# All chunks of an mLSTM moved from among the linear-attention tiles to among the later projection pairs, with six more SBUF units for temporaries

## The chip, the cores and the metric

The kernel runs on one core of one Trainium2 chip. The metric is device time in microseconds (us): the median of 3 runs. Besides, one execution was profiled; durations below come from that one. Engines are named as in the profile: PE (TensorE matmul), PEld (its weight loads), DVE (VectorE), ACT (ScalarE), POOL (GpSimd) and SP (SyncE, which issues every DMA here).

## The reference, cut to what matters

One decoder layer over 2048 tokens and 1024 channels. One wide input projection feeds four token mixers that run in parallel; each result is gated, projected back, the four are merged by sigmoid gates and projected out. What is moved here is mixer B, a chunkwise mLSTM with a state carried from chunk to chunk.

```python
u = jnp.einsum('bsd,de->bse', h, w_in)                 # 15 pieces, 8720 columns
y_a = rg_lru(xa, ...) * silu(lru_z)                    # A
...
def step(carry, xs):                                   # B, one chunk
    C, n, m = carry
    ...
    s = jnp.einsum('bhtd,bhsd->bhts', qc, kc) * jnp.exp(Dm - m_row[..., None])
    num = jnp.einsum('bhts,bhse->bhte', s, vc) + w_inter[..., None] * jnp.einsum('bhtd,bhde->bhte', qc, C)
    h = num / jnp.maximum(jnp.abs(den), jnp.exp(-m_row))[..., None]
    C = decay[..., None, None] * C + jnp.einsum('bhs,bhsd,bhse->bhde', w_s, kc, vc)
...
oh = gla_chunkwise(hq, hk, h_i, log_fh)                # C
og = gla_chunkwise(g_q, g_k, g_v, log_gk)              # D
proj = jnp.einsum('bsnw,nwd->bsnd', branches, w_branch)
return jnp.sum(sigmoid(merge) * proj, axis=2) @ w_out
```

## The kernel before, in words

The tokens are done in two halves of 1024. Each half passes through four stages, and a scheduler that works through a priority heap turns the written program into one fixed order for each engine. `prio(off)` makes what is written inside it more urgent by `off` places.

- **Pairs** (`ahead_pairs`). 33 pairs of 128-column tiles of the input projection, each done as seven products of half size (`ip_pair`, matmuls at L423). Every product has 12 matmuls with a 512-wide moving operand; float32 is split into two parts, so its weight tile is rounded on ACT (L417), the remainder is taken on POOL (L418), weight sums are made on DVE (L428) and the seven results are added up on DVE (L432). The table `GORD` sets the order: `g` is a pair of merge gates, `z` a pair of mixer inputs, `r` an RG-LRU pair, `d` decays, `t` a change of ACT's function table, `m` one step of the mLSTM's gate rows (`mlstm_rows`, matmuls at L787). Results go to DRAM (`pdram`, `gdram`, `rdram`).
- **Mixers** (`mixers`). Twelve linear-attention tiles (`gla_tile`, steps 0 to 7 with one head, 8 to 11 with two), each a chain over POOL, ACT, DVE and PE. The value projections (`ip_vals`, L280) and six gates (L268) are written between them. The mLSTM runs beside them: `both` takes 0.65 of a step of the generator `mlstm()` per step of a tile, after `LEAD` = 8 steps ahead. A chunk of 128 tokens has six steps: `scores` (two) and `rest` (four); there are 8 chunks in a half.
- **Merge** (L268, L1319) and **output projection** (L280, L1354). The scheduler draws merge matmuls forward into the gaps of the last tiles.

A chunk's matmuls are q (L863), v (L872), scores (L879), a transpose (L888), the output gate's transpose (L900), numerator (L908, L909), state (L919) and the last transpose (L941). Between them stand DVE steps, among them the mask (L882), the new state (L922), the layer norm (L937) and the last products (L943, L944), and the loads at L844 and L852. `bank8` hands products one of 8 PSUM banks in turn, `bank` one of the six that are called `mx`. `self.T()` hands out an SBUF unit of 516 floats from the arena of `NU` units.

Of the kernel before, what the change touches and what calls it, by code (L numbers as in the profile page):

```python
# [15 lines left out]
P = 128  # L16
# [4 lines left out]
U = 516  # L21
NU = 16
NA = 4
NY = 8
NP = 6
NE = 5
EPS = 1e-6
NPB = 2
NG = 10
PRE = (("mx", 4), ("mo", 4), ("mz", 4), ("hq", 4), ("hz", 4), ("gz", 4), ("gq", 2), ("gk", 2))  # L30
RATE = 0.65
LEAD = 8
LIM = 10
NTH = 0
RMS = 0
NW = 6
DG = (0,1)
NT = 16
SI = 6
RLAT = 2000  # L40
LAT = -600
GORD = [('g',2),('r',1),('z',1),('g',1),('z',1),('r',1),('g',1),('z',2),('r',1),('g',1),('z',2),('r',1),('z',6),('g',3),('t',0),('m',0),('g',1),('m',0),('g',1),('m',0),('g',1),('m',0),('d',0),('m',0),('g',99),('d',1),('z',2)]
NORM = {"hz": "hnw", "gz": "gnw"}
# [104 lines left out]
class Trunk:  # L148
    def __init__(self, ctx, tc, a, out, dbg=None):
        self.tc, self.nc, self.a, self.out, self.dbg = tc, tc.nc, a, out, dbg or {}  # L150
        nc = self.nc
        self.const = ctx.enter_context(tc.tile_pool(name="const", bufs=1))
        self.psum = ctx.enter_context(tc.tile_pool(name="psum", bufs=1, space=bass.MemoryType.PSUM))
        self.dram = ctx.enter_context(tc.tile_pool(name="dram", bufs=1, space=bass.MemoryType.DRAM))
        c = self.const
        self.hh = [c.tile([P, HT], F32R, name=f"hh{k}") for k in range(KT)]
        self.hl = [c.tile([P, HT], F32R, name=f"hl{k}") for k in range(KT)]
        self.wr = [c.tile([P, 528], F32, name=f"wr{k}") for k in range(3)]
# [9 lines left out]
        self.mi = 0  # L168
        self.ydram = [self.dram.tile([4, P, HT], F32, name=f"y{n}") for n in range(4)]
# [27 lines left out]
    def free(self, *aps):  # L197
        self.ar.free(*aps)

    def pbank(self):  # L200
        self.bi += 1
        return self.pb[self.bi % NPB]

    def bank(self):
        self.mi += 1
        return self.mx[self.mi % (8 - NPB)]

# [31 lines left out]
    def wpieces(self, aps):  # L239
        nc = self.nc  # L240
        r = []
        with self.prio(self.EV):
            for ap in aps:
                w = ap.shape[-1]
                i = self.wi
                self.wi += 1
                raw, hi, lo = self.wr[i % 3][:, :w], self.wh[i % NW][:, :w], self.wl[i % NW][:, :w]
# [46 lines left out]
    def ip_tok_k(self, pieces, evac, ks):  # L294

        vs = [p[:, 0:256].unsqueeze(1) for p in [self.pbank() for _ in range(NPB)] + [self.bank() for _ in range(8 - NPB)]]
# [99 lines left out]
    def bank8(self):  # L396
        self.gi += 1
        return (self.pb + self.mx)[self.gi % 8]

    def ip_pair(self, t0, t1, fin, first=False):  # L400
# [5 lines left out]
        with self.prio(self.EV):  # L406
            b11, b12, b22 = (r[:, :512] for r in self.wr)
# [56 lines left out]
    def ahead_pairs(self):  # L464
# [71 lines left out]
        r = [lru(j) for j in range(4)]  # L536
        rows = (i for h in range(2) for i in self.mlstm_rows(h, temp))
        first = True
        for n, i in GORD:
            if n == "t":  # L540
                self.exp_ln()
            elif n == "m":
                with self.prio(RLAT):
                    next(rows, None)
            if n in "tm":
# [6 lines left out]
        assert not g and not z and not r and next(rows, 1)  # L552

# [276 lines left out]

    def mlstm(self):

# [9 lines left out]
        def load(n, c):  # L842
            t = self.T()
            nc.sync.dma_start(h4(t), self.pdram[n][:, :, c * 128:(c + 1) * 128].rearrange("h p t -> p h t"))  # L844
            return t

        def loads(c):
            g, cc = divmod(c, 4)
            r = []
            for i in range(2):  # L850
                t = self.T()
                nc.sync.dma_start(h4(t), self.rdram[g][i][:, cc * 128:(cc + 1) * 128].partition_broadcast(P))  # L852
                r.append(t)
            return [load("xm", c), load("mx", c)] + r

        def scores(c, xm, mx, r1b, wib):
# [5 lines left out]
            for h in range(4):  # L862
                T.matmul(ps[:, h * 128:(h + 1) * 128], self.mqk[:, h], h4(xm)[:, h], start=True, stop=True)  # L863
            q, qw = self.T(), wib
# [3 lines left out]
            va = self.T()  # L868
            va3 = h4(va, 129)
# [17 lines left out]
            for h in range(4):  # L887
                T.transpose(ps[:, h * 128:(h + 1) * 128], h4(xm)[:, h], self.cs("id"))  # L888
            xs = self.T()
# [4 lines left out]
        def rest(c, xm, E, qw, va, xs, mo, z):  # L894
            emc = self.mcols[c // 4][:, c % 4, 2]
# [5 lines left out]
            so = mo  # L901
            hm = self.T()
            A.activation(hm[:, :512], po, AF.Copy)
# [20 lines left out]
            self.free(E, qw, va, xs)  # L924
            yield
            V.tensor_tensor(den, den, emc, op=ALU.max)
# [21 lines left out]

        ld = loads(0)
        nxt = yield from scores(0, *ld)  # L950
        for c in range(8):
            cur = nxt
            mz = [load("mo", c), load("mz", c)]
            if c < 7:
                nxt = yield from scores(c + 1, *loads(c + 1))
            yield from rest(c, *cur, *mz)

# [230 lines left out]
    def mixers(self):  # L1188
# [4 lines left out]
        self.gates_ahead(next(fill))  # L1193
        other = self.mlstm()
        due = 0.0

        def both(gen):

            nonlocal due
            for _ in iter(lambda: next(gen, 1), 1):  # L1200
                due += RATE
                while due >= 1:
                    due -= 1
                    next(other, None)

        with mix():
            for _ in range(LEAD):
                next(other, None)
        hv = self.ip_vals(0, 256)
# [14 lines left out]
        for s, (j, gi) in enumerate(steps):  # L1224
# [15 lines left out]
            with mix():  # L1240
                if j < 4:
                    both(self.gla_tile(2, gi, [j], *x, [hv[j][gi]], zs, [(0, 128)], self.S[j], self.eps_h))
                else:
                    p = j - 4
                    both(self.gla_tile(3, gi, [2 * p, 2 * p + 1], *x, gd[p][gi], [v[gi] for v in gv[2 * p:2 * p + 2]], zs,
                                       [(0, 64), (64, 64)], self.S[j], self.eps_g))
        with mix():
            for _ in other:
                pass
        self.ar.base, self.ar.lim = 0, None  # L1250
# [298 lines left out]
```

## Time and profile before

| what | us |
|---|---|
| median of 3 runs | 2728.09 (2724.17 to 2729.37) |
| the profiled execution, its own time | 2737.6 |
| its span, from the first to the last instruction | 2735.8 |
| pairs, first half, 54 to 747 | 693.0 |
| pairs' end to the first tile's states (L1058) | 39.4 |
| from there to the eighth tile's | 232.3 |
| from there to the twelfth tile's | 152.9 |
| from there to the end of the merge | 118.4 |

A matmul's recorded time includes its way through the array, so PE reads as busy over a stall that is shorter than that way. The "granted clock" is the share of TensorE's full rate that the chip allowed in a stretch; 1.00 is 2.4 GHz throughout, and each part of the time at the other level, 1.2 GHz, lowers the mean.

### The profile page before, as it was taken

To read this page: it belongs to the slowest core of one execution; us is meant where nothing else is said; L and a number is where in the kernel's file an instruction comes from. 1 tells how busy PE (TensorE), PEld (TensorE's weight loads), DVE (VectorE), ACT (ScalarE), POOL (GpSimd) and SP (SyncE) were. 2 spreads that over 40 slices of the span, in tenths; PEclk is the share of its full clock that TensorE was granted. 3 is DMA by queue.
4 is the path that set the end of the run, shared out by engine and by line. 5 is a ranking of instruction groups with operands and counts; after the bars stand their busy time and mean duration, and the time that the engine had idled before them with its cause. 6 is when DMAs were issued, how large, how long until landed. Compare 5 with 4: busy or idle time off the path is not lost. (4 is left out here: it accounts for less than half of the span.)

```text
span 2735.8 us, 45795 instructions
## 1 busy us (share of the span) xinstructions
PE 2604.2 (95%) x16800; PEld 2155.0 (79%) x16800; DVE 1739.0 (64%) x2907; ACT 1296.8 (47%) x2769; POOL 1500.4 (55%) x1273
## 2 busy tenths in 40 slices
PE   7999999999998898999999999999999999999999
PEld 5777878878788886778977777788787888776789
DVE  8787676447667778634376957754657667775332
ACT  5455444434444464452454454454345455644533
POOL 5566556444555555466475566554445555654753
PEclk9999999999999998999999999999999989999999
DMA  6233223443454336785442432243346433558721
GB/s 227 70 127 104 85 85 131 135 135 112 156 178 126 103 123 205 271 288 160 140 139 77 140 115 85 89 131 124 123 131 203 129 106 120 183 168 289 260 95 74
DMA packets 227073, 393.03 MB, mean 144 GB/s; under 512 B 20721, under 2 KB 78081, under 8 KB 226849
## 3 DMA queue, kind: packets, MB, share of 16 engines
q1 hardware_dynamic: 226848, 390.11, 43.2%
q8 instruction: 132, 2.16, 0.3%
q14 instruction: 93, 0.75, 0.1%
HBM read 270.42 MB, written 119.60 MB: 143 GB/s over the span
## 5 line engine op out<-in xcount | busy, mean ns | idle before, releaser
L418 POOL TENSOR_TENSOR wl<-wr,wh 128x512 fp32r<-128x512 f32 x264 | 370.2, 1407 | 300.5 <-ACT wh L417 292.2
L418 POOL TENSOR_TENSOR wl<-gth,wh 128x512 fp32r<-128x512 f32 x198 | 286.4, 1447 | 280.7 <-ACT wh L417 266.7
L423 PE MATMUL mx<-s,wh 128*128 128x512 f32 x1248 | 395.0, 396 | 5.5 <-DVE arena L432 2.4
L432 DVE TENSOR_TENSOR arena<-arena,mx 128x512 f32<-128x512 f32 x386 | 252.8, 681 | 184.4 <-PE mx L423 168.1
L250 POOL TENSOR_TENSOR wl<-wr,wh 128x512 fp32r<-128x512 f32 (+1 forms) x176 | 248.5, 1420 | 194.1 <-ACT wh L249 159.3
L423 PE MATMUL mx<-hh,wl 128*128 128x512 f32 x824 | 328.1, 398 | 9.4 <-POOL wl L418 9.4
L423 PE MATMUL mx<-hh,wh 128*128 128x512 f32 x824 | 326.8, 397 | 5.8 <-DVE mqk L624 3.6
L423 PE MATMUL mx<-hl,wh 128*128 128x512 f32 x824 | 327.5, 397 | 2.4 <-DVE hl L306 2.3
L268 PE MATMUL pb<-hh,wh 128*128 128x512 f32 x704 | 291.0, 415 | 11.4 <-DVE lw L1319 4.0
L268 PE MATMUL pb<-hl,wh 128*128 128x512 f32 x704 | 287.6, 409 | 3.2 <-DVE hl L1293 3.2
L268 PE MATMUL pb<-hh,wl 128*128 128x512 f32 x704 | 286.5, 407 | 0.0
L423 PEld LDWEIGHTS mx<-s,wh 128*128 128x128 f32 x1248 | 235.7, 189 | 62.7 <-DVE arena L432 2.8
L417 ACT ACTIVATE wh<-wr 128x512 fp32r<-128x512 f32 x264 | 164.2, 627 | 229.0 <-PE mx L423 142.6
L280 PE MATMUL pb<-wh,hh 128*128 128x256 f32 (+1 forms) x880 | 254.2, 290 | 3.6 <-DVE lrt L1125 2.3
L280 PE MATMUL pb<-wl,hh 128*128 128x256 f32 (+1 forms) x880 | 253.9, 289 | 1.7 <-POOL wl L250 1.7
L280 PE MATMUL pb<-wh,hl 128*128 128x256 f32 (+1 forms) x880 | 253.5, 288 | 0.0
L423 PE MATMUL mx<-s,wl 128*128 128x512 f32 x624 | 245.5, 397 | 0.0
L417 ACT ACTIVATE wh<-gth 128x512 fp32r<-128x512 f32 x198 | 124.3, 628 | 228.5 <-DVE gth L428 184.4
L423 PEld LDWEIGHTS mx<-hh,wl 128*128 128x128 f32 x824 | 155.8, 189 | 51.5 <-POOL wl L418 16.0
L423 PEld LDWEIGHTS mx<-hh,wh 128*128 128x128 f32 x824 | 156.4, 190 | 46.3 <-issue 7.0
L249 ACT ACTIVATE wh<-wr 128x512 fp32r<-128x512 f32 (+1 forms) x176 | 110.2, 629 | 165.0 <-PE pb L268 110.1
L423 PEld LDWEIGHTS mx<-hl,wh 128*128 128x128 f32 x824 | 155.9, 189 | 41.1 <-DVE hl L306 3.6
(614 smaller groups left out, 6081.8 us busy)
## 6 DMA issues: line engine op xcount, KB each, us to landing
wr<-in_wc_dram SPq DMA_DIRECT2D x246, 256.0 KB, 2.7
g<-arena SPq DMA_DIRECT2D x52, 512.0 KB, 3.4
gth<-in_wc_dram SPq DMA_DIRECT2D x66, 256.0 KB, 2.8
wr<-in_wb_dram SPq DMA_DIRECT2D x64, 256.0 KB, 3.3
hl<-y SPq DMA_DIRECT2D x32, 512.0 KB, 5.9
arena<-g SPq DMA_DIRECT2D x48, 256.0 KB, 4.5
arena<-in_xT_dram SPq DMA_DIRECT2D x32, 256.0 KB, 5.2
lw<-g SPq DMA_DIRECT2D x32, 256.0 KB, 3.6
```

The costliest lines, as they stand in the source:

```text
L249: nc.scalar.activation(hi, raw, AF.Copy)
L250: nc.gpsimd.tensor_tensor(lo, raw, hi, op=ALU.subtract)
L268: nc.tensor.matmul(ps, w[:, ws], h[:, ts], start=(k == 0 and i == 0), stop=(k == nk - 1 and i == 2))
L280: self.nc.tensor.matmul(v, h[:, cs], w[:, ws], start=(first and i == 0), stop=(last and i == 2))
L417: A.activation(hi, w, AF.Copy)
L418: G.tensor_tensor(lo, w, hi, op=ALU.subtract)
L423: nc.tensor.matmul(ps, wp[:, ws], xp, start=(k == 0 and i == 0), stop=(k == 3 and i == 2))
L432: V.tensor_tensor(o, x, y, op=ALU.add)
```

## The change

The mLSTM generator is advanced inside `ahead_pairs` by new `c` entries of `GORD` (48 steps in all, that is every step of a half's 8 chunks), after the first two steps of gate rows; ten of the 33 pairs come after the first `c`. `mixers` runs the tiles alone. From the first `c` on, the products rotate through five banks (`fast`) and the chunks through three (`slow`). Units above `NG` = 10, which hold the temporaries in the pairs, grow from 6 to 12; the space comes from `dynamic_dma_scratch_size=1024`. A fourth raw weight buffer `wr` is added. `NT` falls from 16 to 10, so six gates a half get their tanh in the merge and not in the pairs. The chunk's six steps are put together anew: chunk c's first step is written before the last two of chunk c - 1.

```diff
-NU = 16
+NU = 22
+NF = 3
-RATE = 0.65
-LEAD = 8
+NR = 4
-NT = 16
+NT = 10
-GORD = [('g',2),...,('z',6),('g',3),('t',0),('m',0),('g',1),('m',0),('g',1),('m',0),('g',1),('m',0),('d',0),('m',0),('g',99),('d',1),('z',2)]
+GORD = [('g',2),...,('z',6),('t',0),('m',0),('g',1),('m',0),('g',1),('m',0),('c',2),('g',1),('m',0),('c',4),('d',0),('m',0),('c',4),('g',1),('c',5),('g',1),('c',5),('d',1),('c',5),('g',1),('c',5),('g',1),('c',5),('g',1),('c',5),('z',1),('c',4),('z',1),('c',4)]
...
-        return self.mx[self.mi % (8 - NPB)]
+        return self.slow[self.mi % len(self.slow)]
...
-        return (self.pb + self.mx)[self.gi % 8]
+        return self.fast[self.gi % len(self.fast)]
...
+            elif n == "c":
+                self.fast, self.slow = self.pb + self.mx[:NF], self.mx[NF:]
+                with self.prio(RLAT):
+                    for _ in range(i):
+                        next(chunks)
...
-        ld = loads(0)
-        nxt = yield from scores(0, *ld)
+        last = None
         for c in range(8):
-            cur = nxt
-            mz = [load("mo", c), load("mz", c)]
-            if c < 7:
-                nxt = yield from scores(c + 1, *loads(c + 1))
-            yield from rest(c, *cur, *mz)
+            first = scores(c, *loads(c))
+            next(first)
+            yield
+            if last:
+                yield from last
+            cur = yield from first
+            last = rest(c, *cur, load("mo", c))
+            next(last)
+            yield
+            next(last)
+            yield
+        yield from last
...
-                    both(self.gla_tile(2, gi, [j], *x, [hv[j][gi]], zs, [(0, 128)], self.S[j], self.eps_h))
+                    self.run(self.gla_tile(2, gi, [j], *x, [hv[j][gi]], zs, [(0, 128)], self.S[j], self.eps_h))
...
-    nc = bacc.Bacc("TRN2", target_bir_lowering=False, num_devices=1)
+    nc = bacc.Bacc("TRN2", target_bir_lowering=False, num_devices=1, dynamic_dma_scratch_size=1024)
```

PE's order before, shortly after the first half's last pair, where value projections (L280) and the first chunks stand together; `ma` and `mb` are units that exist only after the pairs:

```order
L280 MATMUL pb_97<-wh_85,hl_75 128x256
L863 MATMUL mx_100<-mb_3_5089,mqk 128x128 x4
L888 MATMUL mx_103<-cst,mb_3_5089 128x128 x4
L280 MATMUL pb_97<-wh_85,hh_68 128x256
L280 MATMUL pb_97<-wl_91,hh_68 128x256
L872 MATMUL mx_101<-mwv,mb_4_5090 128x128
L879 MATMUL mx_104<-mb_0_5086,ma_3_5082 128x128 x4
L872 MATMUL mx_101<-mwv,mb_4_5090 128x128 x3
```

PE's order of the change, late in the pairs; lines have moved on, so L428 is the pairs' product (L423 before), L891 scores (L879), L954 the last transpose (L941), L884 v (L872):

```order
L428 MATMUL mx_102<-s_8_588,wh_83 128x512 x2
L428 MATMUL mx_102<-s_8_588,wl_89 128x512
L428 MATMUL mx_102<-s_9_589,wh_83 128x512
L891 MATMUL mx_103<-arena 128x128
L954 MATMUL mx_105<-cst,arena 128x128 x4
L891 MATMUL mx_103<-arena 128x128 x2
L884 MATMUL mx_104<-mwv,arena 128x128 x4
L891 MATMUL mx_103<-arena 128x128
```

The chunks' groups have moved from the value projections into the products, and use banks 103 to 105 alone.

DVE's order before, in the mixers, where tile steps (L1015 to L1103) and chunk steps (L937, L943, L944) alternate:

```order
L1016 TENSOR_TENSOR mb_5_5091<-mb_5_5091,arena 128x32x8
L1053 TENSOR_TENSOR mb_3_5089<-mb_3_5089,arena 128x512
L937 TENSOR_SCALAR ma_0_5079<-ma_0_5079,mmu_224,mvar_212 128x128 x4
L1103 TENSOR_TENSOR arena<-mx_103,arena 128x512
L1019 COPY_PREDICATED mb_5_5091<-cst,mx_99 128x128
L943 SCALAR_TENSOR_TENSOR mb_3_5089<-mx_100,pvt,mb_3_5089 128x128 x4
```

DVE's order of the change, late in the pairs (L437 adds a product up, L433 is a weight sum, L934 the new state, L950 the layer norm, L956, L896, L957 and L902 the chunk's L943, L884, L944 and L890):

```order
L934 SCALAR_TENSOR_TENSOR Cst_177<-Cst_178,mdec_219,mx_105 128x129 x2
L950 TENSOR_SCALAR arena<-arena,mmu_227,mvar_215 128x128 x4
L437 TENSOR_TENSOR arena<-arena,mx_100 128x512
L433 TENSOR_TENSOR wr_79<-wr_80,wr_79 128x512
L437 TENSOR_TENSOR arena<-arena,mx_101 128x512
L433 TENSOR_TENSOR gth_96<-wr_81,wr_79 128x512
L433 TENSOR_TENSOR wr_80<-wr_81,wr_80 128x512
L956 SCALAR_TENSOR_TENSOR arena<-mx_105,pvt,arena 128x128 x4
L896 TENSOR_TENSOR arena<-arena,mx_103 128x512
L957 TENSOR_TENSOR arena<-arena 128x512
L437 TENSOR_TENSOR arena<-arena,pb_98 128x512 x2
L902 TENSOR_TENSOR arena<-mx_104,mcols_211 128x512
```

The same chunk steps now stand between the pairs' additions and weight sums and no longer between tile steps.

## Rows read from the trace of the kernel before

**Rows 1.** The page, busy time of each engine, share of the span and count.

```profile
PE 2604.2 (95%) x16800; PEld 2155.0 (79%) x16800; DVE 1739.0 (64%) x2907; ACT 1296.8 (47%) x2769; POOL 1500.4 (55%) x1273
```

**Rows 2.** Windows, first half: stretch, us, busy us (count) PE, PEld, DVE, ACT, POOL, clock, DMA.

```profile
54.00:747.00 693.00, 676.24 (x2870) 536.81 (x2870) 465.12 (x623) 324.62 (x525) 377.55 (x274) 0.99 0.33 112
747.00:786.40 39.40, 30.86 (x330) 29.99 (x328) 27.54 (x68) 17.00 (x43) 18.45 (x19) 0.91 0.71 222
786.40:1018.70 232.30, 213.12 (x2208) 192.02 (x2206) 166.91 (x414) 124.15 (x381) 126.57 (x137) 0.98 0.41 122
1018.70:1171.60 152.90, 140.56 (x1587) 109.04 (x1585) 109.36 (x192) 70.97 (x192) 78.37 (x82) 0.93 0.68 233
1171.60:1290.00 118.40, 115.26 (x533) 92.66 (x532) 43.70 (x58) 48.46 (x95) 82.45 (x62) 1.00 0.68 227
```

**Rows 3.** Windows, second half, the same stretches from the pairs' end on.

```profile
2099.00:2135.80 36.80, 29.51 (x317) 28.22 (x316) 25.14 (x63) 14.76 (x40) 17.02 (x19) 0.95 0.69 208
2135.80:2369.70 233.90, 219.95 (x2253) 198.62 (x2251) 169.10 (x418) 125.75 (x390) 128.21 (x138) 0.95 0.40 121
2369.70:2526.80 157.10, 143.23 (x1554) 111.00 (x1553) 105.90 (x189) 73.19 (x187) 80.92 (x81) 0.92 0.68 234
2526.80:2636.00 109.20, 108.61 (x498) 87.06 (x498) 36.57 (x52) 44.62 (x86) 78.23 (x59) 1.00 0.58 195
```

**Rows 4.** PE groups, 54 to 747: count, busy, mean ns, idle before them.

```profile
L423 PE MATMUL mx<-hh,wl 128*128 128x512 f32 x412 | 164.4, 399 | 4.8 <-POOL wl L418 4.8
...
L787 PE MATMUL pb<-arena,gv 128*36 128x512 f32 x16 | 7.8, 601 | 0.0
```

**Rows 5.** PE groups, 747 to 1200: matmuls of the mLSTM.

```profile
L872 PE MATMUL mx<-mwv,ma 128*128 128x128 f32 x32 | 6.0, 349 | 2.2 <-DMA ma<-pmx 2.2
L908 PE MATMUL mx<-ma,arena 128*128 128x129 f32 x24 | 5.3, 307 | 0.3 <-DVE mb L884 0.3
L863 PE MATMUL mx<-ma,mqk 128*128 128x128 f32 x32 | 5.3, 319 | 4.7 <-DMA ma<-pxm 4.7
...
L888 PE MATMUL mx<-cst,ma 128*128 128x128 f32 x16 | 2.9, 311 | 6.5 <-DMA ma<-pxm 6.5
```

**Rows 6.** The same view, 2099 to 2552.

```profile
L863 PE MATMUL mx<-ma,mqk 128*128 128x128 f32 x32 | 6.3, 359 | 8.1 <-DMA ma<-pxm 8.1
...
L863 PE MATMUL mx<-arena,mqk 128*128 128x128 f32 x8 | 1.2, 288 | 0.1
```

**Rows 7.** Timeline of PE: start, us, and count of like matmuls in a row.

```profile
762.99 1.06 PE L863 MATMUL mx<-mb,mqk 128*128 128x128 f32 x8
763.88 0.60 PE L888 MATMUL mx<-cst,mb 128*128 128x128 f32 x4
764.24 0.36 PE L280 MATMUL pb<-wh,hh 128*128 128x256 f32 x1
```

**Rows 8.** The chain that ended last: one unbroken run of merge matmuls.

```profile
2551.89 73.10 PE pb L268 x315
```

**Rows 9.** All groups by line: a pair's additions and weight sums on DVE.

```profile
L432 DVE TENSOR_TENSOR arena<-arena,mx 128x512 f32<-128x512 f32 x386 | 252.8, 681 | 184.4 <-PE mx L423 168.1 <-issue 9.5 <-ACT arena L792 5.5
...
L428 DVE TENSOR_TENSOR wr<-wr,wr 128x512 f32<-128x512 f32 x132 | 97.8, 741 | 77.4 <-POOL wl L418 53.4 <-DMA wr<-in_wc_dram 21.1 <-issue 2.8
...
L428 DVE TENSOR_TENSOR gth<-wr,wr 128x512 f32<-128x512 f32 x66 | 65.6, 995 | 1.2
```

**Rows 10.** The same view: the gates' tanh and a table load on ACT.

```profile
L1309 ACT ACTIVATE arena<-arena 128x512 f32<-128x512 f32 x48 | 30.0, 629 | 52.7 <-DMA arena<-g 52.5
...
L752 ACT ACT_TABLE_LOAD x8 | 10.3, 1283 | 0.1
```

**Rows 11.** DVE groups, 747 to 1200: steps of the mLSTM.

```profile
L922 DVE SCALAR_TENSOR_TENSOR Cst<-Cst,mdec,mx 128x129 f32<-128x129 f32 x32 | 9.6, 339 | 0.0
L937 DVE TENSOR_SCALAR mb<-mb,mmu,mvar 128x128 f32<-128x128 f32 x20 | 9.1, 513 | 3.2 <-ACT mvar L934 3.1
```

**Rows 12.** Waits of SP's queue, 560 to 747: us in total, times, longest.

```profile
SPq L410 <- POOL wl L418: 64.8, 26, 5.5
```

More of the change, by code (lines that the diff above doesn't have):

```diff
@@ L41 @@
 LAT = -600
-GORD = [('g',2),('r',1),('z',1),('g',1),('z',1),('r',1),('g',1),('z',2),('r',1),('g',1),('z',2),('r',1),('z',6),('g',3),('t',0),('m',0),('g',1),('m',0),('g',1),('m',0),('g',1),('m',0),('d',0),('m',0),('g',99),('d',1),('z',2)]
+GORD = [('g',2),('r',1),('z',1),('g',1),('z',1),('r',1),('g',1),('z',2),('r',1),('g',1),('z',2),('r',1),('z',6),('t',0),('m',0),('g',1),('m',0),('g',1),('m',0),('c',2),('g',1),('m',0),('c',4),('d',0),('m',0),('c',4),('g',1),('c',5),('g',1),('c',5),('d',1),('c',5),('g',1),('c',5),('g',1),('c',5),('g',1),('c',5),('z',1),('c',4),('z',1),('c',4)]
 NORM = {"hz": "hnw", "gz": "gnw"}
@@ L157, in __init__ @@
         self.hl = [c.tile([P, HT], F32R, name=f"hl{k}") for k in range(KT)]
-        self.wr = [c.tile([P, 528], F32, name=f"wr{k}") for k in range(3)]
+        self.wr = [c.tile([P, 528], F32, name=f"wr{k}") for k in range(NR)]
         self.wh = [c.tile([P, 528], F32R, name=f"wh{k}") for k in range(NW)]
@@ L168, in __init__ @@
         self.mi = 0
+        self.fast, self.slow = self.pb + self.mx, self.mx
         self.ydram = [self.dram.tile([4, P, HT], F32, name=f"y{n}") for n in range(4)]
@@ L198, in free, with run @@
         self.ar.free(*aps)
+    def run(self, steps):
+        for _ in steps:
+            pass
     def pbank(self):
@@ L246, in wpieces @@
                 self.wi += 1
-                raw, hi, lo = self.wr[i % 3][:, :w], self.wh[i % NW][:, :w], self.wl[i % NW][:, :w]
+                raw, hi, lo = self.wr[i % NR][:, :w], self.wh[i % NW][:, :w], self.wl[i % NW][:, :w]
                 nc.sync.dma_start(raw, ap)
@@ L294, in ip_tok_k @@
     def ip_tok_k(self, pieces, evac, ks):
-        vs = [p[:, 0:256].unsqueeze(1) for p in [self.pbank() for _ in range(NPB)] + [self.bank() for _ in range(8 - NPB)]]
+        vs = [p[:, 0:256].unsqueeze(1) for p in [self.pbank() for _ in range(NPB)] + [self.bank() for _ in self.mx]]
         for k in ks:
@@ L406, in ip_pair @@
         with self.prio(self.EV):
-            b11, b12, b22 = (r[:, :512] for r in self.wr)
+            b11, b12, b22 = (r[:, :512] for r in self.wr[:3])
             b21, w2 = self.gth
@@ L537, in ahead_pairs @@
         rows = (i for h in range(2) for i in self.mlstm_rows(h, temp))
+        chunks = self.mlstm(temp)
         first = True
@@ L544, in ahead_pairs @@
                     next(rows, None)
-            if n in "tm":
+            elif n == "c":
[3 more added lines that the diff above has]
+                        next(chunks)
+            if n in "tmc":
                 continue
@@ L551, in ahead_pairs @@
                 del {"g": g, "z": z, "r": r}[n][:i]
-        assert not g and not z and not r and next(rows, 1)
+        assert not g and not z and not r and next(rows, 1) and next(chunks, 1)
+        self.fast, self.slow = self.pb + self.mx, self.mx
     def setup(self):
@@ L829, in mlstm_rows, with mlstm @@
         self.free(ir, lf, m, b, R)
-    def mlstm(self):
+    def mlstm(self, temp):
         nc = self.nc
@@ L842, in load @@
         def load(n, c):
-            t = self.T()
+            t = temp()
             nc.sync.dma_start(h4(t), self.pdram[n][:, :, c * 128:(c + 1) * 128].rearrange("h p t -> p h t"))
@@ L850, in loads @@
             for i in range(2):
-                t = self.T()
+                t = temp()
                 nc.sync.dma_start(h4(t), self.rdram[g][i][:, cc * 128:(cc + 1) * 128].partition_broadcast(P))
@@ L863, in scores @@
                 T.matmul(ps[:, h * 128:(h + 1) * 128], self.mqk[:, h], h4(xm)[:, h], start=True, stop=True)
-            q, qw = self.T(), wib
+            q, qw = temp(), wib
             A.activation(q[:, :512], ps, AF.Copy, scale=float(128 ** -0.5))
             G.tensor_tensor(qw[:, :512], q[:, :512], wib[:, :512], op=ALU.mult)
-            va = self.T()
+            va = temp()
             va3 = h4(va, 129)
@@ L888, in scores @@
                 T.transpose(ps[:, h * 128:(h + 1) * 128], h4(xm)[:, h], self.cs("id"))
-            xs = self.T()
+            xs = temp()
             V.tensor_tensor(h4(xs), h4(ps), bc(wsc), op=ALU.mult)
@@ L892, in scores, with rest @@
             return xm, E, qw, va, xs
-        def rest(c, xm, E, qw, va, xs, mo, z):
+        def rest(c, xm, E, qw, va, xs, mo):
             emc = self.mcols[c // 4][:, c % 4, 2]
@@ L901, in rest @@
             so = mo
-            hm = self.T()
+            hm = temp()
             A.activation(hm[:, :512], po, AF.Copy)
@@ L924, in rest @@
             self.free(E, qw, va, xs)
+            z = load("mz", c)
             yield
@@ L1193, in mixers @@
         self.gates_ahead(next(fill))
[L1194 to L1208, printed above, removed]
         hv = self.ip_vals(0, 256)
@@ L1241, in mixers @@
                 if j < 4:
-                    both(self.gla_tile(2, gi, [j], *x, [hv[j][gi]], zs, [(0, 128)], self.S[j], self.eps_h))
+                    self.run(self.gla_tile(2, gi, [j], *x, [hv[j][gi]], zs, [(0, 128)], self.S[j], self.eps_h))
                 else:
                     p = j - 4
-                    both(self.gla_tile(3, gi, [2 * p, 2 * p + 1], *x, gd[p][gi], [v[gi] for v in gv[2 * p:2 * p + 2]], zs,
+                    self.run(self.gla_tile(3, gi, [2 * p, 2 * p + 1], *x, gd[p][gi], [v[gi] for v in gv[2 * p:2 * p + 2]], zs,
                                        [(0, 64), (64, 64)], self.S[j], self.eps_g))
-        with mix():
-            for _ in other:
-                pass
         self.ar.base, self.ar.lim = 0, None
```

## The prediction

> **What bounds the kernel now.** I read the page first: PE is busy 95% of the span, its weight loads 79%, and no other engine over 64% [rows 1]. As a stall shorter than a matmul's way through the array does not show there, I went on to the windows by stage [rows 2, 3]. Three things are to be seen in them. In the pairs PE is busy 676.2 of 693.0 us at a clock of 0.99. From the pairs' end to the merge's end it is idle 39.4 - 30.9 = 8.5, 232.3 - 213.1 = 19.2, 152.9 - 140.6 = 12.3 and 118.4 - 115.3 = 3.1 us, 43.1 together, and in the second half 7.3 + 13.9 + 13.9 + 0.6 = 35.7: 78.8 us, all but a few of them while tiles run. And there the clock falls: 0.91, 0.98 and 0.93, then 0.95, 0.95 and 0.92; in the merge it is 1.00 again. So PE sets the pace in the pairs and the merge, and the dependences of tiles and chunks set it between. DVE is at 166.9 / 232.3 = 0.72 of the stretch in which tiles and chunks run together, so the chain has to share it.
>
> Next, who is waited for. In the groups of PE the idle time that ends with a matmul of the mLSTM adds to 20.2 us in the first half (nine groups, from 6.5 down to 0.3) [rows 5] and to 11.3 in the second (seven, from 8.1 down to 0.1) [rows 6]. The largest are loads of a chunk: its units `ma` and `mb` exist only once the pairs are over, so the first chunk's loads start there.
>
> **What moves at no gain.** The chunks' matmuls. Eight follow each other in 763.88 - 762.99 = 0.89 us and four transposes in 764.24 - 763.88 = 0.36 [rows 7]. A chunk has 48 of the first kind and 12 of the second: 6 x 0.89 + 3 x 0.36 = 6.4 us, and 51 us a half. They leave a stage in which PE is late and enter one in which PE is the limit, so they cancel: -51 and +51.
>
> **What is removed.** First, the idle time ahead of these matmuls in the mixers: -20.2 - 11.3 = -31.5 us over both halves. Its lower bound is nothing: a hole that a chunk's matmul ended may then be ended by a tile's.
>
> Second, what DVE and the clock give back. A chunk has 29 DVE instructions; the state's take 0.34 us and the layer norm's 0.51 [rows 11], so at a mean of 0.38, an estimate between these rows and the smaller ones, about 11 us, 88 a half. About three quarters of that lie in the stretch with seven tiles: 65 of DVE's 166.9 us, or 39%. PE's share of the chunks there is some 45 of its 213.1 us, or 21%. DVE's work falls faster than PE's, so a tile's steps come sooner. The clock: the share missing in the head and in the seven-tile stretch is worth 39.4 x 0.09 + 232.3 x 0.02 = 8.2 us and 36.8 x 0.05 + 233.9 x 0.05 = 13.5 us, 21.7 together, if PE then never rests. I take half of it, 11, and a fifth of the remaining idle (78.8 - 31.5 = 47.3), 9: -20 us. Bounds: all of both, -69; and +30, if the tiles, now closer together, wait for each other more (about the 31.5 us that the chunks' holes are worth).
>
> The table of tiles bears this out by a second way. The stretch with four tiles and no chunk has the same DVE share, 0.72 [rows 2]. With 102 us of DVE left, seven tiles would take 102 / 0.72 = 142 us, but PE still has up to 213.1 - 45 = 168 there: PE becomes the limit, not the chain.
>
> **What is added in the pairs.** Waits of a chunk's matmuls, now in PE's queue between products. Nothing in the rows shows a chunk there. The nearest below are the gate rows, run among the pairs in the same way: no idle before them [rows 4]; so 0. Above, the mixers: 20.2 us a half. The late chunks come densest: after the second `d` entry 28 of 48 steps, 4.7 chunks, share five pairs. A pair has 84 products' matmuls at 73.10 / 315 = 0.232 us [rows 8], 19.5 us; with the chunks that is 97 + 30 = 127 us, 27 a chunk. DVE then needs 11 for the chunk and, for 1.07 pairs, seven additions of 0.68 and four sums of 0.74 to 1.0 (8.2 a pair) [rows 9], 8.8: 0.73 of PE's time. At 0.72 the seven-tile stretch kept PE idle 8%. 8% of 127 us is 10, less for the early chunks; but here the other matmuls on hand are products that wait for nothing, so I take 9 us a half, +18. Bounds 0 and 40 a half.
>
> A chunk also puts seven transfers (six loads and the store) on SP's queue, among the weight loads. That queue already waits for POOL to give weight buffers back, 64.8 us in 187 [rows 12], so a chunk's load stands behind a weight load by up to 5.5 us; that is in the upper bound. Behind a blocked load stands the next weight tile, and the POOL remainder that products waited for, 4.8 us in the whole stage [rows 4].
>
> **Banks.** Products now turn through five banks, not eight. A product fills one for 12 x 0.232 = 2.8 us, so the bank comes round after 13.9 us, and its addition takes 0.68; DVE waited 168 us for PE before these additions, and not the other way round [rows 9]. By these rows the cost is 0. The Trainium skill (Perfetto Trace Analysis, Matmul Optimizations) asks that all 8 PSUM banks be used for parallelism; it speaks against this edit, and by it the sum would be that of the fourth rival below.
>
> **Small edits.** Twelve tanh a half go from the pairs to the merge, 0.63 us each on ACT, and the ACT order lists 37 table loads for 35, 1.28 each [rows 10]. ACT is at 0.41 of the merge stretch and 0.47 in the pairs, so PE's work covers both; without that cover, 7.5 + 1.3 us a half. The fourth raw buffer `wr` lets one more weight load start early; the merge has 3.1 and 0.6 us of idle to win from, so 0. The smaller scratch serves no transfer here, as all come from SP: 0.
>
> **Sum.** -31.5 - 20 + 18 = -33.5 us. The profiled execution's own time is 2737.6 (span 2735.8 and 1.8 around it): 2704.1. The median of the runs shown is 2728.09, 0.9965 of it, so 2695.
>
> **Rivals.** (1) The chunks stall the products. Each has ten bank fillings and only three banks, q, scores, numerator and state wait for ACT and DVE in turn, and PE takes its queue in order. At 5 us a chunk, 40 a half, the sum is -31.5 - 20 + 80 = +28.5: 2757. For it: DVE's 0.73 above. Against: the gate rows' 0.0. It decides from 26 us a half on. Chance 0.10.
>
> (2) The tiles' own chains keep the pace. Then the mixers shrink by the 51 us alone, holes pass to other matmuls, and the pairs' 18 us remain: +18, 2746. For it: four tiles without a chunk still idle 12.3 and 13.9 us at 0.93 and 0.92. Against: the seven-tile stretch's DVE, above. Chance 0.10.
>
> (3) All comes back: -31.5 - 47.3 - 21.7 and only 4 us in the pairs: -96, 2632. For it: the pairs' 2.4% idle with other mixed work in them. Against: the tile chains stay. Chance 0.10.
>
> (4) Five banks bind. Ten pairs a half come after the first `c`, 70 products; if each waited for one addition of 0.68 us, that is 95 us over both halves: -51.5 + 18 + 95 = +61.5, 2789. Chance 0.03.
>
> That the change would not do what it says is excluded by the order: the chunks' last transpose stands before the first half's last product on PE.
>
> **How the numbers follow.** The forecast has 0.67; its own range is 2661 to 2727: from -31.5 - 40 + 4 = -67.5 to -20 - 5 + 24 = -1. The range 2640 to 2748 leaves out rival 1, rival 4 and half of rival 3: 0.18. A measurement of this kernel tells about 0.2% from no change, 5.5 us: 2722.6 to 2733.5 counts as the same. Of the forecast 0.07 lies there. Faster: 0.60 + 0.10 = 0.70; slower: 0.10 + 0.10 + 0.03 = 0.23.
>
> **What would show it.** In the profile after: the pairs 693 + 51 + 9 = about 753 us with PE busy over 97% and a clock of 0.99; the first value projection to the merge's end 543 - 51 - 26 = about 466; no wait for a chunk's load in the mixers, the first tile's states within 25 us of the pairs' end (39.4 before); granted clock in the tiles at 0.96 or more. I am wrong if the pairs pass 770 us, or if the stretch from the pairs' end to the merge's end stays above 485; of the first the cause would be PE idle before chunk matmuls (rival 1) or products late after additions (rival 4).

## The result, and the profile after

The change makes the kernel slower: 2820.57 us median (2819.95 to 2821.63) against 2728.73 (2724.17 to 2732.91), ratio 1.0337, interval 1.0319 to 1.0355. The prediction had 2695, at most 2748: sign and range are wrong.

The profiled execution's span is 2818.8 us, 83 more than before. By stage: the start 5 more; the pairs 765 and 749, 72 and 66 more; from the pairs' end to the merge's last product 512 and 509, where it was 543 both times (747 to 1290, 2099 to 2642), 31 and 34 less; between the halves 5 more. Windows of the kernel after by these stages, columns as in [rows 2]; first half to the next half's first product:

```profile
59.00:824.00 765.00, 735.25 (x3348) 592.95 (x3349) 545.25 (x857) 363.22 (x693) 396.18 (x295) 0.98 0.38 122
824.00:837.00 13.00, 9.11 (x103) 8.71 (x102) 13.00 (x16) 3.28 (x6) 11.37 (x10) 0.88 0.71 269
837.00:1047.00 210.00, 183.85 (x2004) 165.26 (x2004) 131.10 (x250) 97.13 (x252) 122.54 (x133) 0.92 0.26 84
1047.00:1177.00 130.00, 115.38 (x1398) 88.19 (x1397) 82.49 (x158) 64.08 (x172) 60.13 (x63) 0.86 0.60 203
1177.00:1336.00 159.00, 151.11 (x666) 120.20 (x665) 55.91 (x73) 61.66 (x115) 96.68 (x73) 0.97 0.69 225
1336.00:1467.00 131.00, 120.03 (x876) 112.78 (x874) 70.31 (x114) 62.16 (x151) 65.51 (x59) 0.99 0.43 147
...
1467.00:2216.00 749.00, 728.76 (x3340) 588.38 (x3341) 525.99 (x818) 360.42 (x690) 399.92 (x297) 0.99 0.39 125
2216.00:2231.00 15.00, 9.06 (x103) 8.73 (x102) 13.04 (x17) 3.54 (x7) 14.49 (x10) 0.85 0.72 259
2231.00:2444.00 213.00, 181.52 (x2000) 162.45 (x1999) 134.55 (x258) 97.89 (x256) 127.33 (x135) 0.91 0.27 85
2444.00:2573.00 129.00, 113.80 (x1419) 87.36 (x1417) 81.00 (x154) 62.30 (x168) 56.35 (x62) 0.91 0.62 211
2573.00:2725.00 152.00, 145.79 (x653) 116.06 (x653) 50.97 (x69) 61.22 (x115) 97.39 (x72) 0.99 0.60 200
```

Read the third row against its counterpart in [rows 2]. The seven tiles lost some 45 us of PE work by the prediction's estimate, and 36 us of DVE work, yet took 210 us in place of 232, with PE idle 26 us and the clock at 0.92 where it was 0.98. DVE is down to 131.1 / 210 = 0.62, so its amount of work is not the limit. PE still waits for it: 25 of the 26 us end with a DVE step, so DVE is the last link of chains that are late for another reason. The page's engine row says of the whole that PE is busy 19 us more, in a span 83 longer.

```profile
PE 2622.9 (93%) x16800; PEld 2169.1 (77%) x16800; DVE 1772.9 (63%) x2907; ACT 1301.9 (46%) x2771; POOL 1514.6 (54%) x1273
```

What SP's queue waits for from the pairs' end to the eighth tile, 824 to 1047 (us in total, times, longest). L718 loads a tile's four inputs, L253 the weights:

```profile
SPq L253 <- POOL wl L255: 37.9, 18, 9.9
SPq L718 <- PE mx L1098: 24.3, 1, 24.3
SPq L718 <- DVE S L1090: 20.0, 1, 20.0
```

The second is a load that waits for a unit that the output products of the tile before (L1098) still read, the third one for a unit that a state update (L1090) uses. Nothing is issued behind such a load: at the longer one, SP issues nothing from 980.82 to 1005.45. But PE is idle only 4 us from 980 to 1010, so the longest waits are not the dearest. What such a wait does behind the queue is seen best at a shorter one:

```profile
890.74 0.33 SPq L718 DMA_DIRECT2D arena<-phz  x1
899.06 0.32 SPq L718 DMA_DIRECT2D arena<-phf  x1
900.51 0.32 SPq L718 DMA_DIRECT2D arena<-phg  x1
905.16 0.32 SPq L718 DMA_DIRECT2D arena<-phz  x1
915.47 1.61 SPq L253 DMA_DIRECT2D wr<-in_wt_dram  x2
```

and POOL's of the same time:

```profile
903.40 1.49 POOL L988 TENSOR_SCALAR mb<-arena 128x512 f32<-128x512 f32 x1 [3.47 <-DMA arena<-phg]
...
913.96 2.76 POOL L255 TENSOR_TENSOR wl<-wr,wh 128x528 fp32r<-128x528 f32 x2
```

The load of `phf` stands 8 us for its unit; `phg` goes out behind it at 900.51, and POOL waits for it until 903.40. Behind the tile's POOL steps stands the remainder of two weight tiles of the value projection (913.96), for which SP's next weight load waits until 915.47. Two queues kept in order thus tie a projection, which needs no tile, to a tile's input. PE loses 16 of its 26 idle us between 900 and 940:

```profile
900.00:940.00 40.00, 24.28 (x266) 22.86 (x265) 27.84 (x41) 14.44 (x37) 24.45 (x28) 0.80 0.24 74
```

Its longest wait there, 8.2 us, goes back to a unit too, but to a store and not to a load:

```profile
927.51 0.69 DVE L1122 TENSOR_TENSOR arena<-mx,arena 128x512 f32<-128x512 f32 x1 [5.09 <-PE mx L1121]
928.23 0.33 SPq L1125 DMA_DIRECT2D y<-arena  x1
930.31 1.22 DVE L987 TENSOR_TENSOR_SCAN arena<-cst,mb 128x512 f32<-128x512 f32 x1 [2.11 <-DMA y<-arena]
935.64 0.65 PE L1012 MATMUL mx<-arena 128*32 128x32 f32 x32 [8.18 <-DVE arena L1035]
```

A tile's result (L1122) is stored (L1125); the first DVE step of a later tile (L987) waits for that store, whose unit it takes over (the trace names the pool and not the unit), and PE has nothing to do until that tile's first products (L1012). So units that loads and temporaries take from one pool in turn can delay the tiles in two ways: in SP's queue, and directly.

### The profile page after: what moved, and what is told of

Read it like the earlier page. It is cut to its first block, busy times and chain, and to the rows that moved or that the text cites. A ratio compares the mean times of both kernels' runs of the same rounds, so it can differ in the third digit from the quotient of the medians.

```text
span 2818.8 us, 45721 instructions
## 1 busy us (share of the span) xinstructions
PE 2622.9 (93%) x16800; PEld 2169.1 (77%) x16800; DVE 1772.9 (63%) x2907; ACT 1301.9 (46%) x2771; POOL 1514.6 (54%) x1273
## 5 line engine op out<-in xcount | busy, mean ns | idle before, releaser
L423 POOL TENSOR_TENSOR wl<-wr,wh 128x512 fp32r<-128x512 f32 x264 | 373.1, 1419 | 332.1 <-ACT wh L422 317.5
L423 POOL TENSOR_TENSOR wl<-gth,wh 128x512 fp32r<-128x512 f32 x198 | 288.9, 1459 | 288.2 <-ACT wh L422 267.0
L428 PE MATMUL mx<-s,wh 128*128 128x512 f32 x1104 | 354.0, 399 | 9.7 <-ACT s L310 4.5
L428 PE MATMUL mx<-hh,wh 128*128 128x512 f32 x776 | 310.9, 401 | 12.9 <-DVE mcols L840 5.3
L428 PE MATMUL mx<-hh,wl 128*128 128x512 f32 x776 | 310.9, 401 | 6.6 <-POOL wl L423 6.6
L428 PE MATMUL mx<-hl,wh 128*128 128x512 f32 x776 | 311.0, 401 | 2.2 <-DVE hl L311 2.2
L437 DVE TENSOR_TENSOR arena<-arena,mx 128x512 f32<-128x512 f32 x346 | 227.2, 679 | 116.4 <-PE mx L428 99.4
L428 PEld LDWEIGHTS mx<-s,wh 128*128 128x128 f32 x1104 | 208.6, 190 | 61.1 <-DVE s L311 6.4
L428 PE MATMUL mx<-s,wl 128*128 128x512 f32 x552 | 217.9, 398 | 0.0
L273 PEld LDWEIGHTS pb<-hh,wh 128*128 128x128 f32 x704 | 138.8, 198 | 62.9 <-DVE lw L1320 12.8
L428 PEld LDWEIGHTS mx<-hh,wh 128*128 128x128 f32 x776 | 148.6, 191 | 48.8 <-DVE mcols L840 5.8
L285 PEld LDWEIGHTS pb<-wh,hh 128*128 128x128 f32 x880 | 170.9, 195 | 16.4 <-DVE arena L1142 9.6
```

The lines of the kernel that those rows point to most:

```text
L273: nc.tensor.matmul(ps, w[:, ws], h[:, ts], start=(k == 0 and i == 0), stop=(k == nk - 1 and i == 2))
L285: self.nc.tensor.matmul(v, h[:, cs], w[:, ws], start=(first and i == 0), stop=(last and i == 2))
L423: G.tensor_tensor(lo, w, hi, op=ALU.subtract)
L428: nc.tensor.matmul(ps, wp[:, ws], xp, start=(k == 0 and i == 0), stop=(k == 3 and i == 2))
L437: V.tensor_tensor(o, x, y, op=ALU.add)
```

## The experiments

Times are medians in us; behind them stands the ratio to the kernel before, or its 95% interval. That kernel was measured anew beside each, at 2729 to 2733 us. "Mixers" is short for pairs' end to merge's last product.

**What the chunks and the banks cost in the pairs.** First the chunks left out:

```diff
-                    for _ in range(i):
-                        next(chunks)
+                    pass
```

> The changed kernel with the chunks left out altogether: no mLSTM output is computed, its branch is fed with a copy of another path; banks, buffers and the order of the pairs stay as changed. If the pairs' 72 and 66 us are all the chunks' own work and waits, the pairs fall back to 693 and 683 us and the time to 2820 - 138 = about 2682 us. If the five banks, the smaller units or the denser order cost the products something, the pairs stay above 705 us each and the time above 2705. The mixers hold no chunk in either kernel, so both expect 512 and 509 us there from the pairs' end to the merge's end.

2704.08, ratio 0.9901 (0.9884 to 0.9917). The pairs take 701 and 689 us, so a half's chunks cost 64 and 60 there: 51 of work by the prediction's estimate, and 13 and 9 more. Of these PE shows 4 a half as idle (29.8 against 25.4 us, and 20.2 against 15.8); the rest lies within its busy time. But 8 and 6 us above the kernel before are not the chunks'. Then this without the split of the banks:

```diff
-                self.fast, self.slow = self.pb + self.mx[:NF], self.mx[NF:]
```

> The changed kernel without chunks (the mLSTM left out, as in the first experiment) and without the split: products turn through eight banks. The pairs of that experiment took 701 and 688 us, 8 and 5 more than before. If five banks cost that, they fall to 693 and 683: 2704 - 13 = 2691. If it is the order of the pairs or chance, they stay: 2700 to 2708.

2673.70 (0.9781 to 0.9824): 30 us faster, and the pairs 690 and 677. The five banks cost the products 11 and 12 us in the two halves; the other 7 lie outside the pairs, where both turn through the same banks. More than half of the cost is a single wait in each half, 6.9 and 6.8 us, of a product for ACT to copy out its bank (L443), which is not there with eight banks:

```profile
PE pb L428 <- ACT arena L443: 6.9, 1, 6.9
```

With the chunks in, no product of the first half waits so long (2.2 us at most), so what the five banks cost beside chunks is not measured by itself. And the changed kernel, chunks in, with the same line taken out:

> The changed kernel without the split of the banks: products turn through all eight, chunks through the six that they share. If five banks bind, the pairs lose the 15 to 21 us a half that lie above the chunks' own work and the time falls to about 2785 us. If the chunks' own waits are the cause, a shared bank takes nothing off them, and products now wait for banks that a chunk holds: 2815 to 2850.

2864.46 (1.0470 to 1.0508), pairs 783 and 767. A chunk that shares banks with the products waits for their additions (L437) and, once, for a load:

```profile
PE mx L883 <- DVE arena L437: 12.2, 3, 11.3
PE mx L911 <- DMA arena<-pmo: 6.0, 1, 6.0
```

So the split is the lesser evil, but not free. The pairs' windows, first without chunks and with five banks, then without chunks and with eight, then with chunks and eight:

```profile
60.00:761.00 701.00, 675.58 (x2865) 536.26 (x2866) 468.45 (x624) 317.30 (x516) 374.98 (x271) 0.98 0.35 116
...
1409.00:2098.00 689.00, 673.22 (x2860) 534.96 (x2861) 445.40 (x589) 314.97 (x514) 379.19 (x274) 0.99 0.36 119
```

```profile
59.00:749.00 690.00, 674.37 (x2868) 535.98 (x2869) 467.63 (x623) 317.63 (x517) 376.26 (x271) 0.99 0.36 118
1390.00:2067.00 677.00, 669.05 (x2858) 532.60 (x2859) 443.61 (x590) 314.66 (x513) 380.09 (x274) 0.99 0.37 121
```

```profile
60.00:843.00 783.00, 734.90 (x3318) 589.95 (x3319) 530.48 (x833) 359.99 (x674) 393.81 (x294) 0.97 0.37 119
```

**What the mixers are without chunks.** The kernel before, its chunks left out and nothing else:

```diff
-        other = self.mlstm()
+        other = iter(())
```

> The kernel before with the chunks left out: no mLSTM output is computed, its branch is fed with a copy of another path. Nothing else differs in sizes, so this is what the mixers are without chunks. By the prediction they give back the chunks' 51 us of PE work, the holes of their loads and part of the rest, 77 us a half: 2730 - 154 = 2576. If the tiles' own chains keep the pace and the holes only pass to other matmuls, 25 to 35 us a half: 2660 to 2680.

2630.45 (0.9622 to 0.9654). The mixers shrink by 52 and 51 us, which is the chunks' PE work and nothing more. PE is idle 41 us in the first half's mixers and 40 in the second's; with the chunks it was 43 and 36:

```profile
749.00:777.00 28.00, 19.12 (x243) 17.99 (x242) 26.32 (x34) 10.38 (x19) 25.55 (x22) 0.92 0.41 149
777.00:950.00 173.00, 169.33 (x1865) 150.64 (x1866) 120.50 (x240) 90.11 (x246) 115.09 (x127) 0.97 0.31 96
950.00:1111.00 161.00, 140.66 (x1543) 109.27 (x1542) 90.72 (x168) 72.38 (x180) 71.50 (x69) 0.94 0.69 235
1111.00:1240.00 129.00, 120.87 (x547) 96.67 (x547) 45.45 (x59) 49.65 (x95) 83.99 (x61) 0.96 0.60 196
```

Neither theory had this number. The seven tiles do shrink to 173 us, near the 168 of PE's work that the prediction left them, but the stretches behind them grow by 8 and 11. And the changed kernel's mixers, with the same work for PE, take 21 and 17 us more than these.

**The small sizes.** The kernel before with all three (22 units, four raw buffers `wr`, the smaller scratch), then with one of the first two, the scratch in both:

```diff
-NU = 16
+NU = 22
...
-        self.wr = [c.tile([P, 528], F32, name=f"wr{k}") for k in range(3)]
+        self.wr = [c.tile([P, 528], F32, name=f"wr{k}") for k in range(4)]
```

> The kernel before with the changed kernel's sizes alone: 22 units, four raw weight buffers, the smaller scratch. If these are free, 2728 us (within 5). If they bring the 5 us at the start and the 4 us in the middle, 2737.

> The kernel before with four raw weight buffers and the smaller scratch, 16 units. Of the 54 us that all three sizes cost together, the theory that the units are the cause gives this one the 8 us at the start at most: 2728 to 2738. If the fourth buffer lets weight loads run ahead of the tiles' loads in the queue, it has most of it: 2765 or more. If the smaller scratch were the cause, this and the next kernel would both be late by 40 us.

> The kernel before with 22 units and the smaller scratch, three raw buffers. The pool hands out units in turn, so six more change which earlier work a unit waits for and with it the order of the tiles on every engine (1133 of 2505 rows of DVE stand elsewhere). If that is where the 54 us come from: about 2728 + 46 = 2774, all of it between the pairs' end and the first product of the next half. If the raw buffer is the cause: 2730.

All three: 2784.66 (1.0170 to 1.0221), 54 us for sizes that do no work. Four buffers: 2758.93 (1.0071 to 1.0129). 22 units: 2769.77 (1.0116 to 1.0161). Both theories were too simple, as each has a part. The smaller scratch is in all three and was not run alone; if the parts simply add up, it holds about 10 us. The units' loss lies in the mixers, 561 us in each half, and not in the pairs:

```profile
749.00:1310.00 561.00, 505.17 (x4636) 427.43 (x4635) 342.22 (x720) 264.01 (x709) 302.61 (x297) 0.95 0.54 173
2118.00:2679.00 561.00, 509.71 (x4648) 433.01 (x4647) 348.75 (x724) 266.49 (x711) 307.62 (x298) 0.93 0.51 164
```

The changed kernel with three raw buffers (`NR = 3`):

> The changed kernel with three raw weight buffers again. If the fourth buffer costs nothing but the late start: 2812 to 2820. If it holds back the tiles' or the chunks' loads: below 2800. If the chunks need it in the pairs, as their loads stand in the weight queue: above 2830.

2819.60: its products start 6 us earlier, and the stretch between the halves is 6 shorter; pairs and mixers take both back. And the kernel before with `NT = 10`:

> The kernel before with one number changed: the tanh of gates 10 to 15 runs in the merge, as in the changed kernel. If PE's work covers it, as the prediction had it, 2728 us. If the merge's second branch waits for it, as 8 to 12 us of PE idle before the products of gates 10 to 15 suggest, 2728 + 2 x 10 = about 2748 us.

2736.56 (1.0012 to 1.0044), 6 to 8 us; its mixers still take 543 and its span is 2 us below that of the kernel before, so the profiled execution doesn't show where.

**More work among the tiles.** Eight half gates more a half:

```diff
+            if s in (1, 2, 3, 5, 6, 8, 9, 10):
+                self.gate(10 + s // 2, (s % 2,))
```

> The changed kernel with eight more half gates among the tiles of each half, 48 products' matmuls of 0.232 us for two, so some 45 us of PE work a half more (gates that the pairs have computed already, computed once more: work doubled, the values the same). If PE sets the pace of the tiles, the time grows by all of it: 2820 + 89 = 2909. If the tiles' chain sets it and PE has holes to fill, by less than half: below 2865.

2906.26 (1.0630 to 1.0678), 86 us more: all of it, as if PE set the pace. But its windows show where it went: the tiles' stretches take 219 and 127 us, the last one 189 where it was 159.

```profile
839.00:1058.00 219.00, 198.65 (x2085) 175.94 (x2085) 136.15 (x250) 100.87 (x262) 136.03 (x142) 0.95 0.29 92
1058.00:1185.00 127.00, 116.63 (x1412) 89.16 (x1411) 79.74 (x150) 71.51 (x182) 68.07 (x66) 0.91 0.49 162
1185.00:1374.00 189.00, 176.72 (x780) 139.66 (x781) 62.35 (x84) 67.95 (x122) 100.03 (x76) 0.97 0.73 242
```

From the eighth tile on, the merge's first products fill PE between the tiles; gates put there push them to the end. It doesn't tell the theories apart.

**The loads.** The changed kernel with twelve units for the tiles' loads, in three sets by turns (`T(lo, hi)` takes a unit from that part of the pool), the temporaries in the other 34:

```diff
+            at = 4 * (s % 3), 4 * (s % 3) + 4
...
-        t = self.T()
+        t = self.T(lo, hi)
...
+        self.ar.base = 12
```

> The changed kernel with twelve units kept for the tiles' loads, three sets of four in turn, so that no load waits for a unit that the tile just before is still using. If the loads that stand in the queue until a unit is free (24.3 and 20.0 us the longest) hold back the weights behind them and so the tiles, the mixers shrink by 20 us a half or more: 2780 or less. If the tiles' own chain is the limit: 2800 to 2830, with those waits gone.

2760.09 (1.0100 to 1.0134): 60 us of the 92 are gone. The mixers take 475 and 473 us, some 69 less than before; the first half's, but for their last 2 us:

```profile
830.00:856.00 26.00, 17.85 (x205) 17.14 (x203) 25.42 (x35) 9.57 (x17) 20.85 (x22) 0.80 0.38 127
856.00:1028.00 172.00, 166.94 (x1909) 148.72 (x1908) 120.88 (x233) 89.56 (x243) 113.68 (x120) 1.00 0.33 103
1028.00:1157.00 129.00, 116.64 (x1422) 89.51 (x1421) 82.62 (x153) 72.49 (x178) 57.83 (x60) 0.89 0.60 204
1157.00:1303.00 146.00, 139.95 (x633) 111.43 (x632) 50.34 (x70) 56.86 (x110) 93.15 (x71) 1.00 0.71 240
```

The seven tiles take 172 us with PE busy 97%, at full clock: PE is idle 5 us there, 26 without these units, and no step of DVE, POOL or ACT waits for a store. The loads' own waits in SP's queue do not go away. From the pairs' end to the eighth tile they add to 88 us, where they were 117; the longest single one is 14, where it was 24:

```profile
SPq L718 <- DMA y<-arena: 14.9, 8, 3.9
SPq L718 <- DVE mb L995: 13.9, 1, 13.9
```

So if the tiles lose by the turn of the units, the queue is only one of its ways, and the runs do not part them. A chance effect of the new order was the rival. So the same twelve units kept from the temporaries but used by nothing, and the loads' own units in two sets (`s % 2`):

> The changed kernel with the same twelve units kept from the tiles' temporaries as in the experiment with the loads' own units, but used by nothing: the loads take their turn among the other 34. If the loads' waits in the queue are what that experiment took away, they are back here and the time with them: 2800 or more. If the other turn of the temporaries and the order that follows from it did it, this one has it too: about 2760.

> The experiment with the loads' own units, but two sets of four in place of three, the temporaries' units the same: a tile's loads now wait until the tile before last is wholly done. If the place of the loads in the queue sets the pace, the mixers lose a good part of the 38 us a half again: 2785 or more. If it does not, 2755 to 2765.

2843.51 (1.0386 to 1.0430) and 2816.21 (1.0284 to 1.0326), 83 and 56 us above the run with three sets. In the first the loads also take their turn among the 34 units, so the temporaries have fewer. In the second the temporaries have the same 34 to themselves, and only the number of sets differs. Three sets and three raw buffers, then four sets (`s % 4`, so 30 units for the temporaries):

> The experiment with the loads' own units and three raw weight buffers. The fourth cost 6 us at the start of the products in every kernel that had it, and nothing else is known of it here: 2760 - 6 = 2754. If the tiles' order falls out worse by chance, as it did with small changes to the kernel before, 2770 or more.

> The experiment with the loads' own units, four sets of four in place of three, so the temporaries turn through 30 units instead of 34. Two sets took 2816 and three 2760. If the loads still wait for units with three sets, a fourth brings more: 2745 or less. If with three they are early enough, 2755 to 2770; above that, the temporaries run short.

2767.08 and 2804.15. The first gains nothing by its earlier start; with four sets the seven tiles are quick (177 us), but the four behind them take 155, as with two sets, and not 128. That the temporaries run short there is argued, not shown. Six units set aside while the mixers run, the loads in turn with the rest:

> The changed kernel with six units set aside while the mixers run, so that the tiles turn through 40 units, as in the kernel before. If the wider turn is what the mixers lose by, they shrink by the 20 to 25 us a half that the sizes cost the kernel before: 2820 - 45 = 2775. If a tile without chunks beside it is bound by its own chain, or any other order is as bad: 2810 to 2830.

2810.36 (1.0254 to 1.0304): seven tiles in 191 us, the four behind them in 168. The loads' own units in the kernel before, with 22 units:

> The kernel before, its chunks among the tiles, with 22 units, the smaller scratch and the loads' own twelve units. With 22 units alone it took 2770. If the loads' waits in the queue cost there what they cost the changed kernel, 30 us a half, this one falls to 2710 and beats both; if the loss of the 22 units is one of order alone, it stays between 2745 and 2790.

2757.37 (1.0072 to 1.0109), 12 less than with 22 units alone, and 27 more than the kernel before. There the chunks' loads, without units of their own, stand in the same queue; that they hold it up was not tried. Last, the loads' own units with six banks for the products and two for the chunks (`NF = 4`):

> The experiment with the loads' own units, and six banks for the products and two for the chunks in place of five and three. Without chunks, eight banks in place of five brought the products 11 and 10 us a half; with chunks in the same banks they cost 19 and 18. If the products need the sixth bank more than a chunk its third: the pairs fall by 5 us or more, 2750 or less. If a chunk's fillings in two banks wait for each other: the pairs grow by 20 us or more a half, 2800 or more.

2784.67 (1.0179 to 1.0213). The pairs do fall, to 762 and 745 us from 771 and 754, but the mixers grow to 500 and 492: the order has changed behind them. Which part of that is the banks' is open.

## Why the prediction was wrong, by its own steps

**What moves at no gain: right.** 51 us a half is what the mixers lose without chunks (52, 51), and the larger part of what the pairs grow by with them (64, 60).

**What is added in the pairs: right in kind and near in size.** 18 us forecast, 22 measured, as the pairs' growth beyond 51 a half; the idle time of PE that the prediction had in mind is 4 a half of it.

**What is removed: the step that failed.** First, the 31.5 us of holes ahead of the chunks' matmuls were taken as gained. Without chunks the kernel before gives back its PE work alone, and PE is idle 81 us in the mixers of both halves where it was 79, so other matmuls took the holes over; it was the lower bound that the step named. Second, the 20 us from DVE's share and the clock. The seven tiles do come near the forecast pace when nothing else is in their way (173 and 172 us against 168 of PE's work), so the argument from DVE held for that stretch; but the kernel before without chunks pays a part back behind them, and the changed kernel never has it. There the units come round in another turn, and tiles wait for units that earlier loads and stores still hold: in SP's queue, and in DVE's first step of a tile. Together the two terms were to bring 51.5 us; the kernel before without chunks brings 1 beyond the chunks' 102, and the changed kernel loses 37. The prediction read SP's queue in the pairs alone [rows 12], not in the mixers, whose chunks it took away. By its own test (mixers above 485 us) it is wrong: 512 and 509. The first tile's states do come 13 and 15 us after the pairs' end, within its 25, but the clock in the seven tiles is 0.92 and 0.91, not 0.96. For the mixers rival 2, that they shrink by 51 alone, was nearest, and still 17 to 21 us a half too kind. Rival 4 has the nearest time, 2789, but not the reason: it priced the banks at 95 us.

**Banks: priced at 0, measured at 23.** The argument that DVE waits for PE, and not the other way round [rows 9], goes by totals, and in these a single wait of 6.9 us, for ACT and not for DVE, is not seen. The Trainium skill (Perfetto Trace Analysis, Matmul Optimizations) asks that all 8 PSUM banks be used for parallelism. The runs without chunks agree: eight in place of five are worth 30 us, 23 of them in the pairs. With chunks the rule doesn't choose, as either way all eight are in use, split or shared; the split is faster by 44 us.

**Small edits: priced at 0.** In the kernel before, the sizes alone cost 54 us. They add no work; they change which unit, and so which earlier reader, each tile waits for, and with 22 units 1133 of 2505 rows of DVE's order stand in another place, as the expectation above has counted. In the changed kernel, units for the loads took back 60.

**The sum as measured**, in us over both halves.

- The pairs: 102 of work, 22 beyond it, 23 for the banks, and 9 less because without chunks and with eight banks they take 690 and 677 us in place of 693 and 683: 138.
- The mixers: 103 less without chunks, and 38 back, the difference between the changed kernel and the kernel before without chunks: -65. The loads' own units take 74 off the changed kernel's mixers, so the turn of the units is enough to account for the 38.
- The start and the stretch between the halves: 10, which three raw buffers take away.

Together 83, by which the profiled executions differ. With the loads' own units the mixers give back 69 us a half, near the 77 forecast. The change is still slower, by 31 us in the medians and 18 in the profiled executions: its pairs take 149 us more, and not the 120 of the prediction. What is left open is why each size costs the kernel before what it does; its order changes on every engine, and no run here holds that order fixed.

## What to carry to other kernels

Work that leaves a stage gives back its own time on the bound engine; expect no more, as the holes ahead of it here passed to whatever came next. A run of the old kernel without that work shows it before anything is moved. Before moving work, run the change's buffer sizes alone: a pool handed out in turn ties each load and each temporary to an earlier reader. Where loads share an in-order queue with weights, try units of their own: three sets deep brought the changed kernel 60 us, two sets 4, and the kernel before stayed slower with them. A move that needs banks of its own takes them from somebody, and that is a term of the sum.

## What the runs showed of the hardware that was not expected

In this trace TensorE's clock falls right behind PE's holes, and makes them dearer. In the changed kernel PE's starts before 895 lie 0.12 us apart; then it waits 0.38 and 1.48 us for DVE, and from 898.7 on the same matmuls start 0.21 us apart until they come back to 0.12 at 902:

```profile
895.21 0.28 PE L285 MATMUL pb<-wh,hh 128*128 128x256 f32 x1
895.33 0.28 PE L285 MATMUL pb<-wl,hh 128*128 128x256 f32 x1
...
896.38 0.46 PE L1012 MATMUL mx<-mb 128*32 128x32 f32 x32 [0.38 <-DVE mb L1035]
898.32 0.46 PE L1055 MATMUL mx<-arena 128*32 128x32 f32 x16 [1.48 <-DVE arena L1035]
...
899.30 0.41 PE L285 MATMUL pb<-wl,hh 128*128 128x256 f32 x1
899.52 0.41 PE L285 MATMUL pb<-wh,hl 128*128 128x256 f32 x1
...
902.18 0.28 PE L285 MATMUL pb<-wh,hh 128*128 128x256 f32 x1
902.30 0.28 PE L285 MATMUL pb<-wl,hh 128*128 128x256 f32 x1
```

The window of the slow matmuls, columns as in [rows 2], has a granted clock of 0.50; from 890 to 895 and from 902 to 905 it is 1.00:

```profile
898.70:902.00 3.30, 3.30 (x18) 3.29 (x16) 1.73 (x6) 0.61 (x2) 0.56 (x2) 0.50 0.36 103
```

That is the step from 2.4 to 1.2 GHz and back. Over the seven tiles the granted clock is 0.92, against 1.00 with the loads' own units: by an estimate from these rows, 184 us of busy PE at 0.92 hold some 15 us that full clock would save. The Trainium skill (Perfetto Trace Analysis, Matmul Optimizations) says that the matmul engine scales its power by its utilization and that matmuls should run back to back in batches; 0.92 with PE idle 26 us and 1.00 with PE idle 5 agree with it.
